# The second products of a feed-forward layer by seven block products in place of eight

## The chip, the cores and the metric

The kernel runs on one core of a Trainium2 chip. TensorE (PE) multiplies, with its weight loads (PEld) beside it; VectorE (DVE), ScalarE (ACT) and GpSimd (POOL) work on SBUF and PSUM; SyncE (SP) issues the DMAs between DRAM and SBUF. Each engine runs its own row of instructions in order, and semaphores tie the rows together. The metric is the device time of one execution of the whole kernel in microseconds, as the median of several runs.

## The reference

One layer of a model, in float32, for 1024 tokens of width 1024: a mixing block, a cross attention, a gated feed-forward and a last norm. Only the feed-forward and the norm bear on this change:

```python
u = rmsnorm(h, norm_ffn_g[l])
h = h + (jax.nn.silu(u @ ffn_w1[l]) * (u @ ffn_w3[l])) @ ffn_w2[l]
...
return rmsnorm(h, norm_final_g)
```

`ffn_w1` and `ffn_w3` are 1024 by 2816, `ffn_w2` is 2816 by 1024. The products `u @ ffn_w1` and `u @ ffn_w3` are called the first products here, the one with `ffn_w2` the second. Silu is x times sigmoid(x).

## The kernel before

All large products are made of pairs: a float32 block is split in a high part (a copy, rounded to the matmul's format, on ScalarE, L281 in `split`) and a low part (the difference, on POOL, L285, or on VectorE), and `mm3` (L298) issues three matmuls for two such pairs: high by high (L299), high by low (L300) and low by high (L301). A matmul of the feed-forward is 128 by 128 by 512 columns.

The hidden width 2816 is 22 blocks of 128 (`FT`), in two halves of 11 (`HF`). Tokens are two halves of 512, columns of the output two halves of 512.

**First products.** They are made by a scheme of seven block products in place of eight (Strassen's idea in Winograd's form): `products(f, A)` for f = 0 to 10 takes weight blocks of the hidden blocks f and f + 11, forms sums of them on VectorE (L1993 to L1997), and computes seven products (P1, P2, P7, P6, P5, P4, P3), each for both weights, 14 products of 12 matmuls in a step f. Results land in PSUM (one pool of eight banks for everything in the feed-forward, `psum`), and VectorE combines them to four blocks (L1989 to L2018). For f = 0 and 1 two of the products are done earlier and kept in SBUF (tag `kept`, eight buffers). `gated` (L1945) takes a sigmoid (ScalarE, L1949), multiplies (VectorE, L1950) and stores the gated hidden block to the DRAM scratch `hid_d` (SP, L1952), four blocks a step. A step also loads 16 weight tiles of 256 KB into a ring of ten (`raw`, tag `wraw`, L1875); their split parts stand in rings of seven (tags `wh` and `wl`). The five sums of the normed tokens which the products use fill both rings `th` and `tl`, of 20 tiles each, and give them back as the last step's products end.

**Second products.** They run plainly: for each token half h, for each column half c, four PSUM accumulators (tile `acc`, one for 128 tokens each) sum over all 22 hidden blocks; that makes 2 x 2 x 22 x 4 x 3 = 1056 matmuls. Hidden blocks are loaded from `hid_d` once for each h (L2045, into `tl` or, for the last eight, `al`), copied for the high part on ScalarE (L2046) and subtracted for the low part on POOL (L2047). Weights come by `raw`, and are split as before. The last three hidden blocks of a pass are done row tile by row tile (`ILAST`), so that the four accumulators end one after the other. After a pass, VectorE adds accumulator and residual (L2087), ScalarE squares with a sum (L2089), POOL multiplies by the gain (L2091), and after the second column half the norm's factor is made (L2095) and applied (`finish`, L2078 to L2082).

**What sets the order.** A scheduler orders each engine's row by the program's order, by priorities and by a clock that it simulates; so code written late can come early in the rows where its inputs are there. All DMAs spoken of here are issued by SP, in one order, and each waits for the one that was issued eight before it.

Of the kernel before, what the change touches and what calls it, by code (L numbers as in the profile page):

```python
# [183 lines left out]
def tile_trunk(ctx, tc, x, mem, norm_mix_g, w_in, rw_mu, rw_w0, rw_w2, rw_a0, rw_a2, rw_g2,  # L184
# [1686 lines left out]
    hd = scratch("hid_d", [FT, NHALF, P, HALF])  # L1871
    def raw(src, k, c, kn, cn):
# [20 lines left out]

    def blocks():

        return [[fp.tile([P, HALF], F32, tag=t, name=f"h{t}", bufs=4 if t == "s" else 2) for t in ts] for ts in (("u2", "u3"), ("c", "s"))
                for _ in range(2)]
# [47 lines left out]
    def gated(n, C, s, f, t):  # L1945

        if n == 0:
            s = fp.tile([P, HALF], F32, tag="s", name="s", bufs=4)
            nc.scalar.activation(s, C, AF.Sigmoid)  # L1949
        nc.vector.tensor_tensor(s, C, s, op=ALU.mult)  # L1950
        if n:
            nc.sync.dma_start(out=hd[f, t], in_=s)  # L1952
        return s

# [74 lines left out]
    next(late)  # L2029
    for f in range(HF):  # L2030
        products(f, weights(f))

    fg = fp.tile([P, D], F32, name="fg", bufs=1)
    nc.sync.dma_start(out=fg, in_=norm_final_g.partition_broadcast(P))
    order = [f + e for f in range(HF) for e in (0, HF)]
    ILAST = 3
    for h in range(NHALF):
        a = act(act1)
        hid = []
        for n, f in enumerate(order):  # L2040
            if n >= FT - KT:
                hh, hl = (t[:, n - FT + KT, :] for t in a)
            else:
                hh, hl = (ring.tile([P, HALF], F32R, tag=t, name=t) for t in ("th", "tl"))
            nc.sync.dma_start(out=hl.bitcast(F32), in_=hd[f, h])  # L2045
            nc.scalar.activation(hh, hl.bitcast(F32), AF.Copy)  # L2046
            nc.gpsimd.tensor_tensor(hl, hl.bitcast(F32), hh.bitcast(F32), op=ALU.subtract)  # L2047
            hid.append((hh, hl))
        hs = blocks()
        for i in range(4):  # L2050
            for c in range(2):
                nc.sync.dma_start(out=hs[i][c], in_=h2d[(4 * h + i) * P:(4 * h + i + 1) * P, c * HALF:(c + 1) * HALF])
        ss = sp.tile([P, 4, 8], F32, tag="ssf", name="ssf")
        for c in range(2):
            cs = slice(c * HALF, (c + 1) * HALF)
            acc = [psum("acc") for _ in range(4)]
            w2 = []
            for n, f in enumerate(order):
# [66 lines left out]
```

## Time and profile before

| what | value |
| --- | --- |
| median of 3 runs | 2398.14 us (2397.16 to 2399.48) |
| the profiled execution | 2398.55 us, its span 2396.8 us |
| granted TensorE clock | 0.993 |
| TensorE busy | 97% of the span |
| second products, first to last matmul | 2139.3 to 2389.9 us of the span |

A page of the profile gives busy time by engine; a window gives the same for a stretch; a row of a timeline gives start and duration of an instruction and, in brackets, how long its engine was idle before it and what released it. Lines such as L2046 are those of the kernel before.

### The profile page before, as it was taken

How to read it: one execution, taken by the hardware profiler on the slowest of the kernel's cores; microseconds unless marked ns; L12 is line 12 of the kernel's file. 1: busy time of each engine (PE TensorE's matmuls, PEld its weight loads, DVE VectorE, ACT ScalarE, POOL GpSimd, SP SyncE). 2: the span in 40 equal slices, each digit the busy share in tenths (PEclk: the TensorE clock that was granted, in tenths of full speed). 3: DMA queues.
4: the chain of work that ended last, by engine and by line, in shares of the span. 5: the costliest groups of instructions: out<-in, count | busy, mean ns of one | idle time of the engine just before them, and what ended most of it. 6: DMA issues, size and time to landing. Idle time of an engine off the chain costs nothing. (4 is left out here: it accounts for less than half of the span.)

```text
span 2396.8 us, 48780 instructions
## 1 busy us (share of the span) xinstructions
PE 2335.8 (97%) x19258; PEld 1934.3 (81%) x19258; DVE 1411.2 (59%) x2288; ACT 1128.3 (47%) x2249; POOL 1228.8 (51%) x1268
## 2 busy tenths in 40 slices
PE   7999999999999999999998999999999999999998
PEld 5777777778887878888887998889778888877887
DVE  5887874667777667767754525444687565640101
ACT  6545454646566656555663415444433333343332
POOL 3554545555466555665664511112565444477673
PEclk9999999999999999999999999999999999999999
DMA  5444445333344343434244823133723223265441
GB/s 168 122 127 121 123 117 161 74 101 85 92 109 110 82 129 105 123 89 126 56 140 152 300 69 117 53 120 132 259 80 101 84 75 93 71 199 172 158 161 57
DMA packets 386001, 288.46 MB, mean 120 GB/s; under 512 B 106171, under 2 KB 329517, under 8 KB 385773
## 3 DMA queue, kind: packets, MB, share of 16 engines
q1 hardware_dynamic: 383341, 279.58, 39.6%
q0 software_dynamic: 1344, 4.72, 0.5%
q8 instruction: 152, 2.49, 0.4%
q10 hardware_dynamic: 1088, 1.05, 0.1%
q14 instruction: 76, 0.62, 0.1%
HBM read 208.73 MB, written 76.02 MB: 119 GB/s over the span
## 5 line engine op out<-in xcount | busy, mean ns | idle before, releaser
L102 PE MATMUL pproj<-uh,whi 128*128 128x512 f32 x768 | 320.0, 417 | 1.1 <-DVE q L102 1.1
L102 PE MATMUL pproj<-uh,wlo 128*128 128x512 f32 x768 | 300.9, 392 | 2.8 <-POOL wlo L102 2.1
L102 PE MATMUL pproj<-ul,whi 128*128 128x512 f32 x768 | 301.2, 392 | 0.0
L285 POOL TENSOR_TENSOR wl<-wraw,wh 128x512 fp32r<-128x512 f32 x154 | 202.1, 1323 | 133.2 <-ACT wh L281 131.6
L285 POOL TENSOR_TENSOR wlo<-wraw,whi 128x512 fp32r<-128x512 f32 (+1 forms) x86 | 117.9, 1374 | 288.6 <-ACT whi L281 280.7
L102 POOL TENSOR_TENSOR wlo<-wraw,whi 128x512 fp32r<-128x512 f32 x96 | 129.0, 1355 | 118.8 <-ACT whi L102 103.8
L281 ACT ACTIVATE whi<-wraw 128x512 fp32r<-128x512 f32 (+1 forms) x166 | 101.0, 617 | 173.1 <-PE pw L301 62.0
L299 PE MATMUL pproj<-uh,whi 128*128 128x512 f32 (+1 forms) x432 | 179.5, 416 | 0.9 <-ACT whi L281 0.6
L281 ACT ACTIVATE wh<-wraw 128x512 fp32r<-128x512 f32 x154 | 94.3, 627 | 182.2 <-PE P L300 74.5
L301 PE MATMUL pproj<-uh,wlo 128*128 128x512 f32 (+1 forms) x432 | 171.4, 397 | 1.5 <-POOL wlo L285 1.5
L102 PEld LDWEIGHTS pproj<-uh,whi 128*128 128x128 f32 x768 | 144.4, 188 | 34.3 <-DVE q L102 2.4
L300 PE MATMUL pproj<-ul,whi 128*128 128x512 f32 (+1 forms) x432 | 170.7, 395 | 0.0
L102 PEld LDWEIGHTS pproj<-ul,whi 128*128 128x128 f32 x768 | 144.3, 188 | 32.0
L102 PEld LDWEIGHTS pproj<-uh,wlo 128*128 128x128 f32 x768 | 144.9, 189 | 28.1 <-POOL wlo L102 2.5
L285 POOL TENSOR_TENSOR wlT<-wraw,whT 128x512 fp32r<-128x512 f32 x70 | 96.6, 1386 | 96.2 <-ACT whT L281 92.5
L299 PE MATMUL pw<-whi,ah 128*128 128x256 f32 x512 | 144.6, 282 | 0.0
L300 PE MATMUL pw<-wlo,ah 128*128 128x256 f32 x512 | 144.6, 282 | 0.0
L301 PE MATMUL pw<-whi,al 128*128 128x256 f32 x512 | 144.3, 282 | 0.0
L2087 DVE TENSOR_TENSOR hu<-acc,hu 128x512 f32<-128x512 f32 x8 | 5.5, 692 | 200.0 <-PE acc L301 200.0
L285 DVE TENSOR_TENSOR wlo<-wraw,whi 128x512 fp32r<-128x512 f32 x80 | 73.7, 922 | 83.4 <-ACT whi L281 83.1
L102 ACT ACT_TABLE_LOAD x90 | 115.5, 1283 | 13.5 <-DVE m L102 6.4
L299 PEld LDWEIGHTS pproj<-uh,whi 128*128 128x128 f32 (+1 forms) x432 | 81.6, 189 | 25.4 <-issue 6.2
(457 smaller groups left out, 6656.2 us busy)
## 6 DMA issues: line engine op xcount, KB each, us to landing
wraw<-in_ffn_w_dram SPq DMA_DIRECT2D x192, 256.0 KB
wraw<-in_w_in_dram SPq DMA_DIRECT2D x148, 256.0 KB
hid_d<-s SPq DMA_DIRECT2D x44, 256.0 KB
tok<-in_x_dram SPq DMA_DIRECT2D x16, 512.0 KB
ar_d<-AR SPq DMA_DIRECT2D x32, 256.0 KB
bk_d<-BK SPq DMA_DIRECT2D x16, 512.0 KB
AR<-ar_d SPq DMA_DIRECT2D x64, 128.0 KB
BK<-bk_d SPq DMA_DIRECT2D x16, 512.0 KB
```

What stands on the lines that cost most here:

```text
L102: r = getattr(self.engine, op)(*a, **kw)
L281: nc.scalar.activation(hi, src, AF.Copy)
L285: e.tensor_tensor(lo, src, hi.bitcast(F32), op=ALU.subtract)
L299: nc.tensor.matmul(ps, ah, bh, start=first, stop=False)
L300: nc.tensor.matmul(ps, ah, bl, start=False, stop=False)
L301: nc.tensor.matmul(ps, al, bh, start=False, stop=last)
L2087: sums.append(nc.vector.tensor_tensor(o, acc[i], o, op=ALU.add).ins.name)
```

## The change

The second products, too, are made by seven block products. Hidden blocks f and f + 11 are the two halves of the inner dimension, so the operands are two by two: tokens by hidden, hidden by columns. Four sums of the gated hidden blocks are made in each step f (`hidden_sums`) and stored to a new DRAM scratch `hsum_d`; four sums of blocks of `ffn_w2` are made for each f (`weight_sums`) and stored to `wsum_d`. Of the four gated blocks of a step only three are stored themselves now. The pool of the `s` tiles has six buffers, where four were.

```diff
     def gated(n, C, s, f, t):
 
         if n == 0:
-            s = fp.tile([P, HALF], F32, tag="s", name="s", bufs=4)
+            s = fp.tile([P, HALF], F32, tag="s", name="s", bufs=6)
...
         if n:
-            nc.sync.dma_start(out=hd[f, t], in_=s)
+            hid[f, t] = s
+            if (f, t) != (f % HF, 1):
+                nc.sync.dma_start(out=hd[f, t], in_=s)
...
+    def hidden_sums(f):
+        x11, x21, x12, x22 = (hid.pop(k) for k in ((f, 0), (f, 1), (f + HF, 0), (f + HF, 1)))
+        s3 = fp.tile([P, HALF], F32, tag="c", name="S3h")
+        nc.gpsimd.tensor_tensor(s3, x11, x21, op=ALU.subtract)
+        tt(x21, x21, x22, op=ALU.add)
+        tt(x11, x21, x11, op=ALU.subtract)
+        nc.gpsimd.tensor_tensor(x12, x12, x11, op=ALU.subtract)
+        for n, t in enumerate((x21, x11, s3, x12)):
+            nc.sync.dma_start(out=hsd[n, f], in_=t)
+
+    def weight_sums(f):
+        y = {}
+        for r in range(2):
+            for c in range(2):
+                y[r, c] = t = fp.tile([P, HALF], F32, tag="kept", name=f"y{r}{c}", bufs=8)
+                nc.sync.dma_start(out=t, in_=ffn_w2[0, (f + r * HF) * P:(f + r * HF + 1) * P, c * HALF:(c + 1) * HALF])
+        t3 = fp.tile([P, HALF], F32, tag="kept", name="T3w", bufs=8)
+        nc.gpsimd.tensor_tensor(t3, y[1, 1], y[0, 1], op=ALU.subtract)
+        nc.gpsimd.tensor_tensor(y[0, 1], y[0, 1], y[0, 0], op=ALU.subtract)
+        tt(y[1, 1], y[1, 1], y[0, 1], op=ALU.subtract)
+        tt(y[1, 0], y[1, 1], y[1, 0], op=ALU.subtract)
+        for n, t in enumerate((y[0, 1], y[1, 1], t3, y[1, 0])):
+            nc.sync.dma_start(out=wsd[n, f], in_=t)
...
+    summed = iter(range(HF))
     for f in range(HF):
         products(f, weights(f))
+        if f >= AHEAD:
+            for _ in range(2 if f < 2 * AHEAD else 1):
+                weight_sums(next(summed))
+        hidden_sums(f)
```

The loops of the second products become seven passes, each over 11 hidden blocks, with four accumulators: 7 x 11 x 4 x 3 = 924 matmuls. A pass has its hidden operand, its weight operand and what is done with its accumulators. The low part of a hidden block is VectorE's now. The residual is loaded in eight DMAs of 512 KB into the tiles that held `ah` and `al`, which the hidden blocks don't use any more.

```diff
+    def p1(i, acc):
+        nc.scalar.activation(U[i], acc, AF.Copy)
+        more(0, i, 0, U[i])
+
+    def p6(i, acc):
+        tt(U[i], acc, U[i], op=ALU.add)
+
+    def p5(i, acc):
+        tt(V[i], acc, U[i], op=ALU.add)
+        more(0, i, 1, V[i])
+        more(1, i, 1, V[i])
+
+    def p7(i, acc):
+        tt(U[i], acc, U[i], op=ALU.add)
+        more(1, i, 0, U[i])
+        add(1, i, 1, acc, ALU.add, True)
...
+    for x, y, then in ((lambda f: hd[f, 0], w2(0, 0), p1),
+                       (lambda f: hd[f + HF, 0], w2(1, 0), lambda i, acc: add(0, i, 0, acc, ALU.add, True)),
+                       (lambda f: hsd[1, f], wsum(1), p6),
+                       (lambda f: hsd[0, f], wsum(0), p5),
+                       (lambda f: hsd[3, f], w2(1, 1), lambda i, acc: add(0, i, 1, acc, ALU.add, False)),
+                       (lambda f: hsd[2, f], wsum(2), p7),
+                       (lambda f: hd[f + HF, 1], wsum(3), lambda i, acc: add(1, i, 0, acc, ALU.subtract, False))):
+        acc = [psum("acc") for _ in range(4)]
+        ops = []
+        for f in range(HF):
+            hh, hl = (ring.tile([P, HALF], F32R, tag=t, name=t) for t in ("th", "tl"))
+            nc.sync.dma_start(out=hl.bitcast(F32), in_=x(f))
+            nc.scalar.activation(hh, hl.bitcast(F32), AF.Copy)
+            tt(hl, hl.bitcast(F32), hh.bitcast(F32), op=ALU.subtract)
+            ops.append((hh, hl, *operand(y(f), "2")))
```

`more` adds a tile to the residual's on POOL, `add` is the old sum, square and gain of an accumulator, and `finish` stands as before but for one product, which VectorE does for the first token half.

The first place where rows move is SP's row in step 2 of the first products, between its weight loads (`wraw`) and its stores of gated blocks (`s`). Before:

```order
L1952 DMA hid_d_20188<-s_21122 128x512
L1875 DMA wraw_21371<-in_ffn_w3_dram 128x4x128
L1952 DMA hid_d_20188<-s_21250 128x512
L1875 DMA wraw_21665<-in_ffn_w1_dram 128x4x128
L1952 DMA hid_d_20188<-s_21293 128x512
L1875 DMA wraw_21667<-in_ffn_w1_dram 128x4x128
L1875 DMA wraw_21669<-in_ffn_w1_dram 128x4x128
L1952 DMA hid_d_20188<-s_21334 128x512
```

And after the change, from behind the last weight load of w3:

```order
L1976 DMA y00_21741<-in_ffn_w2_dram 128x512
L1983 DMA wsum_d_20190<-T3w_21732 128x512
L1983 DMA wsum_d_20190<-y01_21726 128x512
L1976 DMA y01_21743<-in_ffn_w2_dram 128x512
L1983 DMA wsum_d_20190<-y11_21730 128x512
L1976 DMA y10_21745<-in_ffn_w2_dram 128x512
L1976 DMA y11_21747<-in_ffn_w2_dram 128x512
L1983 DMA wsum_d_20190<-y10_21728 128x512
L1976 DMA y00_22074<-in_ffn_w2_dram 128x512
L1983 DMA wsum_d_20190<-T3w_21749 128x512
L1951 DMA hid_d_20188<-s_21267 128x512
L1983 DMA wsum_d_20190<-y01_21743 128x512
```

Four loads of the first group of weight sums stand just ahead of these rows. The loads and stores of the groups alternate, and stand between the weight loads and the gated blocks' stores; in steps 2, 3 and 4 all eleven groups pass.

The second place is POOL's row at the same steps, where `wl` and so on are low parts of weights. Before:

```order
L285 TENSOR_TENSOR wl22_21338<-wraw_21063,wh22_21337 128x512
L285 TENSOR_TENSOR wl11_21374<-wraw_21357,wh11_21373 128x512
L285 TENSOR_TENSOR wl11_21393<-wraw_21365,wh11_21392 128x512
L285 TENSOR_TENSOR wl12_21412<-wraw_21359,wh12_21411 128x512
L285 TENSOR_TENSOR wl12_21434<-wraw_21367,wh12_21433 128x512
L285 TENSOR_TENSOR wlT3_21465<-wraw_21361,whT3_21464 128x512
```

And after:

```order
L285 TENSOR_TENSOR wl22_21355<-wraw_21081,wh22_21354 128x512
L1978 TENSOR_TENSOR T3w_21732<-y11_21730,y01_21726 128x512
L285 TENSOR_TENSOR wl11_21434<-wraw_21417,wh11_21433 128x512
L1979 TENSOR_TENSOR y01_21726<-y01_21726,y00_21724 128x512
L285 TENSOR_TENSOR wl11_21453<-wraw_21425,wh11_21452 128x512
L285 TENSOR_TENSOR wl12_21472<-wraw_21419,wh12_21471 128x512
L1978 TENSOR_TENSOR T3w_21749<-y11_21747,y01_21743 128x512
L1979 TENSOR_TENSOR y01_21743<-y01_21743,y00_21741 128x512
L285 TENSOR_TENSOR wl12_21494<-wraw_21427,wh12_21493 128x512
L285 TENSOR_TENSOR wlT3_21524<-wraw_21421,whT3_21523 128x512
```

Two sums of each of two groups stand among the low parts there; a sum that waits for its load holds the low parts behind it.

The third place is ScalarE's row at the end of the first products, up to the sigmoid of the last step's C22 (`s`); `th` are high parts of hidden blocks, `wh2` those of `ffn_w2`. Before, the end of that stretch, in which sixteen copies of hidden blocks stand ahead of the sigmoid:

```order
L2046 ACTIVATE th_23875<-tl_23876 128x512
L281 ACTIVATE wh22_23801<-wraw_23527 128x512
L2046 ACTIVATE th_23880<-tl_23881 128x512
L281 ACTIVATE wh2_23942<-wraw_23940 128x512
L2046 ACTIVATE th_23885<-tl_23886 128x512
L2046 ACTIVATE th_23890<-tl_23891 128x512
L281 ACTIVATE wh2_23960<-wraw_23958 128x512
L2046 ACTIVATE th_24794<-tl_24795 128x512
L2046 ACTIVATE th_24799<-tl_24800 128x512
L1949 ACTIVATE s_23714<-C22_23712 128x512
```

And after, where ten stand ahead of it:

```order
L2160 ACTIVATE th_24287<-tl_24288 128x512
L2160 ACTIVATE th_24310<-tl_24311 128x512
L2160 ACTIVATE th_24321<-tl_24322 128x512
L281 ACTIVATE wh22_24052<-wraw_23779 128x512
L281 ACTIVATE wh2_24133<-wraw_24131 128x512
L281 ACTIVATE wh2_24156<-wraw_24154 128x512
L1946 ACTIVATE s_23965<-C22_23963 128x512
```

The last copies stand directly ahead of the sigmoid before, and three weight copies behind the last of them after the change.

129 lines of the change are left out of this document (67 added, 62 removed).

## The prediction

> **What bounds the kernel now.** I read the head of the page first, then the stretches of TensorE, then the waits at the place where the first products of the feed-forward end and the second ones begin, and at last the end of the timeline.
>
> ```profile
> span 2396.8 us, 48780 instructions
> PE 2335.8 (97%) x19258; PEld 1934.3 (81%) x19258; DVE 1411.2 (59%) x2288; ACT 1128.3 (47%) x2249; POOL 1228.8 (51%) x1268
> L2087 DVE TENSOR_TENSOR hu<-acc,hu 128x512 f32<-128x512 f32 x8 | 5.5, 692 | 200.0 <-PE acc L301 200.0
> ```
>
> TensorE is busy 97% of the span, and VectorE waits 200 us of the last stage for TensorE's accumulators. The share is an average, so I ask the stage itself. The first window below holds TensorE's instructions in the first products, the other three those of tile acc alone, which is the second products; the columns are window, sum, busy time with instructions, granted clock, DMA share, GB/s.
>
> ```profile
> core 0: us, PE busy (x), PEclk, DMA share, GB/s
> 1906.80:2098.80 192.00, 192.00 (x841) 1.00 0.27 83
> 2139.30:2186.00 46.70, 39.91 (x168) 1.00 0.65 214
> 2186.00:2382.00 196.00, 196.00 (x856) 1.00 0.39 126
> 2382.00:2389.90 7.90, 7.84 (x34) 1.00 0.20 77
> ```
>
> The first window is five steps f of the first products (a step is 14 products of 12 matmuls, and 5 x 168 = 840), so a step takes 38.4 us at full clock and TensorE has no gap in it. The second products begin at 2139.3 and end at 2389.9. Past 2186 they too have no gap: 196.00 / 856 = 0.2290 us a matmul. Only the first 46.7 us do: 168 matmuls at 0.229 are 38.5 us, so **8.2 us** are lost there. The rows of that place:
>
> ```profile
> ACT th L2046 <- DMA tl<-hid_d: 14.2, 2, 12.0
> PE acc L300 <- POOL wl L285: 3.3, 3, 1.9
> PE acc L299 <- DVE C L2010: 3.3, 1, 3.3
> 2135.26 1.32 ACT L2046 ACTIVATE th<-tl 128x512 fp32r<-128x512 f32 x2 [2.79 <-DMA tl<-hid_d]
> 2136.48 0.61 ACT L1949 ACTIVATE s<-C 128x512 f32<-128x512 f32 x1
> 2137.13 6.47 DVE L1950 TENSOR_TENSOR s<-C,s 128x512 f32<-128x512 f32 x1 [10.19 <-ACT s L1949]
> 2143.52 0.68 DVE L2008 TENSOR_TENSOR U<-P,U 128x512 f32<-128x512 f32 x1
> ```
>
> ScalarE stands in hidden copies (th) that wait for loads; behind them in its row stands a sigmoid (s), on it VectorE's product, and only behind that, at 2143.52, the sum that empties a PSUM bank the new accumulators want. Elsewhere a matmul taken out is worth its 0.229 us.
>
> **The change, term by term.** *Removed:* seven passes of 11 blocks by 4 row tiles by 3 matmuls are 924 matmuls where 1056 stood. 132 x 0.229 = **30.2 us**. All matmuls in it have the same shape, so the price is the row's own.
>
> *The end* keeps its form: last matmul, sum, square, rstd, product, store.
>
> ```profile
> 2389.45 0.40 PE L301 MATMUL acc<-wh,al 128*128 128x512 f32 x1
> 2393.61 0.38 SPq L2082 DMA_DIRECT2D out_dram<-hs  x1
> ```
>
> The last store is issued 3.7 us after the last matmul's end at 2389.9 (2389.45 + 0.40), and the span ends 6.9 us after it. I leave it at 6.9. The profiled execution took 2398.55 us, 1.75 more than its span, and lies 0.41 above the median of the three runs (2398.14), so I count against it. With nothing lost: 2139.3 + 924 x 0.229 + 6.9 + 1.75 = **2359.5**.
>
> *The transition.* ScalarE's row, whose end is shown in the part on the change, has ten hidden copies before the sigmoid of step 10 where sixteen stood, and their low parts are VectorE's now and no longer POOL's (whose wait for wl is the 3.3 us above). Fewer loads must land ahead of the sigmoid; but VectorE takes ten more differences just where it is late. Ten at 0.69 are 6.9 us, spread over the last step. The bounds are 0 and the 8.2 us of now; a loss below zero can't be. The wait was for copies six of which are gone, so I take **2**, nearer to none.
>
> *Evictions and sums between passes.* Of the seven passes, each 132 x 0.229 = 30.2 us, every one leaves four banks while the next uses the other four, so an eviction has a whole pass. POOL has 11 splits at 1.30, 14.3 us, and at most 8 sums at 1.30, 10.4 us: 24.7 of 30.2. VectorE has 11 differences: even at the 1.76 us of a paired one (row below), 19.4 us. ScalarE has 22 copies at 0.66 (1.32 / 2), 14.5 us. Each fits, at 0; if POOL's eight sums after one pass all came ahead of the splits, and none were ready, it would be 10.4 us once. I take 0, for the splits run several operands ahead. The loads are 22 blocks of 0.262 MB in 30.2 us, 191 GB/s, below the 327 shown further down; the residual's eight 512 KB loads stand ahead of the eleventh hidden block, 4.2 MB / 327 = 12.8 us and a landing of 5.4 (also below), 18 us, where the block is needed after 8 x 12 x 0.229 = 22 us. That is 0, and 5 if they land late.
>
> *The sums, in the first products.* A step gets one group of hidden sums (two on POOL, two on VectorE, four stores for one store less), and eleven groups of weight sums (four loads, two POOL, two VectorE, four stores each) are put by the order into steps 2, 3 and 4 and the boundary before them: about four in step 2, three in each of the next. The prices are these:
>
> ```profile
> L1993 DVE TENSOR_TENSOR T<-wraw 128x512 f32<-128x512 f32 x12 | 8.3, 692 | 29.5 <-POOL wl L285 29.5
> L285 POOL TENSOR_TENSOR wl<-wraw,wh 128x512 fp32r<-128x512 f32 x36 | 46.7, 1298 | 52.6 <-ACT wh L281 52.6
> 1783.71 6.39 POOL L285 TENSOR_TENSOR wl<-wraw,wh 128x512 fp32r<-128x512 f32 x4 [3.14 <-ACT wh L281]
> 1779.36 1.76 DVE L1993 TENSOR_TENSOR T<-wraw 128x512 f32<-128x512 f32 x1 [2.94 <-POOL wl L285]
> 1783.76 1.80 DVE L1994 TENSOR_TENSOR wraw<-wraw 128x512 f32<-128x512 f32 x1
> 1786.19 1.07 DVE L1950 TENSOR_TENSOR s<-C,s 128x512 f32<-128x512 f32 x1
> 1787.18 3.47 DVE L1995 TENSOR_TENSOR wraw<-T,wraw 128x512 f32<-128x512 f32 x2
> ```
>
> Alone, VectorE's sum of two SBUF tiles takes 0.69 and POOL's 1.30. Beside each other both get longer: four of POOL take 6.39, **1.60 each**, with four of VectorE among them. Now POOL has 14 splits a step; with 2 hidden and 6 weight sums it is 22, by 1.60 each 35.2 us of 38.4. In step 2, with four groups, 24 x 1.60 = 38.4: full to the brim. VectorE has 16 such sums, then 24, and 14 from PSUM: 38 x 0.69 = 26.2 us if alone. So by paired durations the sums just fit, but the splits have no room left, and a late load moves TensorE. If the pairs took turns entirely, a step would need 22 x 1.30 + 24 x 0.69 = 45.2 us, over by 6.8 in two steps and by 10.7 in step 2, **24 us** in all, less what seven split operands ahead cover (38.4 / 14 = 2.74 us each, 19 us if the ring is full).
>
> The Trainium skill's page "SBUF — State Buffer", section "🔬 SBUF: two separate sides", speaks against this change: it says that a VectorE operation with two SBUF inputs and a GpSimd one that reads SBUF exclude each other for the whole instruction. By that rule the four pairs at 1783.71 would have taken 4 x 1.30 + 4 x 0.69 = 8.0 us; the trace shows 6.39, so it agrees on the lengthening and not on its full size. By the rule the time is that of the crowding rival below, by the trace's pairs that of my forecast.
>
> DMA, in the same steps, by the highest stretch that I find and by now:
>
> ```profile
> core 0: us, PE busy (x) PEld busy (x) DVE busy (x) ACT busy (x) POOL busy (x), PEclk, DMA share, GB/s
> 2270.00:2290.00 20.00, 20.00 (x90) 16.57 (x89) 4.15 (x4) 11.08 (x20) 18.76 (x16) 1.00 0.92 327
> hid_d<-s SPq DMA_DIRECT2D x44, 256.0 KB
> 2149.64 5.39 DMA al<-hid_d
> ```
>
> A step moved 20 blocks of 256 KB (16 loads, 4 stores). Steps 2 to 3 in the new order have 44 between the same places: 44 x 0.262 MB / 38.4 us = 300 GB/s, against 83 now and 327 at a share of 0.92. It fits with little left. I take **2.5 us** for ports and queue together, between 0 and 24, because the pairs' row is the nearest and it says "just fits".
>
> The sum: 2359.5 + 2 + 2.5 = **2364**.
>
> **The rivals.** *Crowding:* the sums take port and queue away from the splits and loads, in steps 2 to 4. For it: 38.4 of 38.4 and 300 of 327. Against: seven operands ahead, and no gap of TensorE in the first products now. Price 5 to 24 us: 2359.5 + 2 + 5 to 24 = 2366 to 2386.
>
> *Slower, by one mechanism:* the weight sums become a chain through their eight buffers. Nine groups have to pass in three steps, 115.2 / 9 = 12.8 us each, or the weight loads behind them on SP come late. One group by itself is a load (5.39, by the landing above), four POOL instructions with splits between (5.2), two paired VectorE sums (3.5), and a store (5.39): 19.5 us. If only one went at a time, nine groups would lose 9 x (19.5 - 12.8) = 60 us less 19 of ring, 41 us: 2361.5 + 41 = 2403, slower than before by over 0.2%. So it decides from about 19.5 us a group. The order speaks against it: the load y00_21741 of the second group stands ahead of the first group's stores, so two are under way, 9.8 us a group.
>
> *No change:* losses of 30 to 40 us, half of that chain, 2394 to 2403. *The change doesn't do what it says:* the order has 924 rows of acc where 1056 were, so this falls out.
>
> **How the numbers follow.** My forecast, 2358 to 2372 (with 0 to 5 at the transition and 0 to 7 in the first products), has 0.62; crowding beyond that, to 2386, 0.24; a better time than 2358, 0.03 (TensorE's matmuls would have to get faster, or the end shorter); between 2386 and 2393, 0.01; within 0.2% of now (4.8 us, about what measurements of this kernel can tell from no change), 0.05; slower 0.05. Faster is thus 0.90. The range runs from 2358 to 2386 and leaves out 0.14.
>
> **What would show it.** In the changed profile, 924 matmuls of acc, nearly 0.229 each, TensorE without gaps past the first 50 us of the second products; the transition's loss 0 to 5 where it was 8.2, with no wait on a C sum's bank over 3 us. Steps of the first products at 38.4 us, also steps 2 to 4; if crowding is right, these alone are longer, TensorE waits there for POOL's wl or for a weight load, and POOL's mean goes over 1.60. For the chain, POOL would stand at T3w waiting for the y loads, ahead of splits. I am wrong if passes of the second products have gaps at their starts (POOL's sums ahead of splits, or hidden blocks that land late), or if TensorE waits at the end of step 10 for more than now.

## The result and the profile after

The change made the kernel slower. Its median is 2412.12 us of 4 runs (2410.04 to 2416.77), that of the kernel before 2397.65 of 4 (2393.81 to 2399.48); the ratio is 1.0065, with a 95% interval of 1.0046 to 1.0085. The prediction had 2364, with a range up to 2386.

The profiled execution is the longest of the four, 2416.77 us, so the stages below add up to 18.2 us more than before, where the medians are 14.5 apart. The head of its page, to be held against the same two lines of before:

```profile
span 2415.0 us, 49046 instructions
PE 2324.8 (96%) x19126; PEld 1919.3 (79%) x19126; DVE 1549.7 (64%) x2425; ACT 1135.5 (47%) x2271; POOL 1265.5 (52%) x1273
```

132 matmuls are gone (19258 to 19126), but TensorE's busy time has fallen by 11 us only, where 132 at 0.229 would be 30. So the matmuls that are left got longer on the average. The stages show where:

| stage, us of the span | before | after | difference |
| --- | --- | --- | --- |
| up to the first acc matmul | 2139.3 | 2179.1 | +39.8 |
| from there to the last one's end | 250.6 | 228.7 | -21.9 |
| from there to the span's end | 6.9 | 7.2 | +0.3 |

The second products did shrink, though by 21.9 us and not by 39 (250.6 less 924 x 0.229). The first products, on which no matmul was changed, take 39.8 us longer. Three windows of TensorE after the change; the first is of all its instructions, the other two of tile acc alone (window, sum, busy time with instructions, granted clock, DMA share, GB/s):

```profile
1820.00:1980.00 160.00, 136.37 (x538) 0.93 0.65 217
```

```profile
2179.10:2300.00 120.90, 120.90 (x534) 1.00 0.69 233
2300.00:2407.80 107.80, 95.21 (x392) 0.94 0.37 122
```

The first window is steps 2 to 5 of the first products. 160 us hold 700 matmuls at 0.2286; there were 538, so 37 us are lost in this window, nearly all of the 39.8. 23.6 of them (160 - 136.37) are idle time, and **13.4** (136.37 - 538 x 0.2286) are matmuls that took longer: the clock fell to 0.93. In the second products there is no loss at their start, where the kernel before had its 8.2; past 2300 TensorE is idle for 12.6 us, with a lower clock again.

What TensorE and its suppliers wait for in the window from 1820 to 1980 (engine, line, what released it: total us, times, longest):

```profile
POOL T3w L1978 <- DMA y<-in_ffn_w_dram: 28.5, 8, 6.3
DVE y L1980 <- POOL y L1979: 21.5, 5, 10.8
PE P L299 <- DVE U L2033: 10.3, 2, 7.8
POOL S3h L1964 <- DVE s L1947: 9.3, 3, 3.2
PE P L301 <- POOL wlT L285: 7.5, 6, 2.5
POOL wl L285 <- ACT wh L281: 6.6, 2, 3.6
POOL s L1967 <- DVE s L1966: 5.9, 4, 1.8
PE P L301 <- POOL wl L285: 5.4, 4, 2.0
```

TensorE waits for POOL's low parts and for a PSUM sum of VectorE's. Both stand behind sums: POOL's row holds at T3w until a block of `ffn_w2` lands, VectorE's at y until POOL has made its sum. An engine that runs ahead waits for its supplier instead; for ScalarE's copies POOL waits 9.0 us only here (6.6 in the row above, 2.4 for whT). In POOL's timeline after the change, such a hold (start, duration, and in brackets the idle time before it and its releaser):

```profile
1826.11 2.54 POOL L285 TENSOR_TENSOR wl<-wraw,wh 128x512 fp32r<-128x512 f32 x2
1834.94 1.29 POOL L1978 TENSOR_TENSOR T3w<-y,y 128x512 f32<-128x512 f32 x1 [6.28 <-DMA y<-in_ffn_w_dram]
1836.19 1.27 POOL L285 TENSOR_TENSOR wl<-wraw,wh 128x512 fp32r<-128x512 f32 x1
```

The blocks land late because their loads go out late. SP stands at the stores of T3w until POOL has made it (first row, of the window from 1815 to 1985), and the next group's loads stand between one group's stores (the other rows):

```profile
SPq L1983 <- POOL T3w L1978: 25.8, 7, 5.1
1838.73 0.33 SPq L1983 DMA_DIRECT2D wsum_d<-y  x1
1839.11 0.42 SPq L1976 DMA_DIRECT2D y<-in_ffn_w_dram  x1
1840.98 0.32 SPq L1983 DMA_DIRECT2D wsum_d<-y  x1
1841.35 0.93 SPq L1976 DMA_DIRECT2D y<-in_ffn_w_dram  x2
```

The T3w of the group whose last loads these are starts at 1845.53. From the third group on, the last load of a group is issued 3.5 to 4.8 us before its T3w starts. So the groups hang together in a chain: a group's last loads wait for stores of the group before, and these for its sums.

### The profile page after: what moved, and what is told of

Same layout as the page of the kernel before. It is cut to its first block, busy times and chain, and to the rows that moved or that the text cites. A ratio compares the mean times of both kernels' runs of the same rounds, so it can differ in the third digit from the quotient of the medians.

```text
span 2415.0 us, 49046 instructions
## 1 busy us (share of the span) xinstructions
PE 2324.8 (96%) x19126; PEld 1919.3 (79%) x19126; DVE 1549.7 (64%) x2425; ACT 1135.5 (47%) x2271; POOL 1265.5 (52%) x1273
## 5 line engine op out<-in xcount | busy, mean ns | idle before, releaser
L2161 DVE TENSOR_TENSOR tl<-tl,th 128x512 fp32r<-128x512 f32 x77 | 80.3, 1069 | 100.5 <-ACT th L2160 96.3
L281 ACT ACTIVATE wh<-wraw 128x512 fp32r<-128x512 f32 x143 | 86.5, 623 | 96.1 <-PE P L300 55.9
L300 PE MATMUL acc<-wl,th 128*128 128x512 f32 x308 | 122.3, 397 | 7.3 <-POOL wl L285 7.3
L299 PE MATMUL acc<-wh,th 128*128 128x512 f32 x308 | 122.0, 396 | 5.2 <-ACT wh L281 5.2
L285 POOL TENSOR_TENSOR wlT<-wraw,whT 128x512 fp32r<-128x512 f32 x70 | 105.3, 1515 | 41.4 <-ACT whT L281 31.0
```

Source lines behind the costliest of these rows:

```text
L281: nc.scalar.activation(hi, src, AF.Copy)
L285: e.tensor_tensor(lo, src, hi.bitcast(F32), op=ALU.subtract)
L299: nc.tensor.matmul(ps, ah, bh, start=first, stop=False)
L300: nc.tensor.matmul(ps, ah, bl, start=False, stop=False)
L2161: tt(hl, hl.bitcast(F32), hh.bitcast(F32), op=ALU.subtract)
```

## The experiments

All of them are kernels of 1 core, each with a profile. "First acc" is the start of the first matmul of the second products, and so where the first products end; "acc" goes from there to the start of the last one; the ideal is 924 x 0.229 = 211.6. The kernel before ran beside each group on the same chip (2399.93; 2395.24; 2397.71; 2395.23; 2396.85). Times of e9, e10 and e15 are medians of several runs, the others single ones. First acc repeats within some 3 us: it is 2179.1, 2176.5 and 2177.4 in the three kernels that have the change's own first products. The whole time repeats less well: 13 executions of the kernel before, beside e9, lie between 2390.79 and 2402.30. So the readings below go by the stages.

| run | sums in the first products | time | first acc | acc |
| --- | --- | --- | --- | --- |
| the change | split between engines, crowded | 2412.12 | 2179.1 | 228.3 |
| e1 | no weight sums | 2374.72 | 2138.6 | 226.7 |
| e2 | arithmetic of the weight sums alone | 2400.08 | 2163.9 | 226.6 |
| e3 | DMAs of the weight sums alone | 2377.25 | 2142.0 | 225.8 |
| e4 | split, spread | 2404.93 | 2154.6 | 241.0 |
| e5 | VectorE, crowded | 2392.25 | 2155.9 | 226.9 |
| e6 | VectorE, spread | 2386.90 | 2143.3 | 234.2 |
| e7 | as the change; residual sums on VectorE | 2406.59 | 2176.5 | 220.8 |
| e8 | e6 and e7 together | 2379.34 | 2144.2 | 225.6 |
| e9 | e8, last group earlier, stores later | 2372.64 | 2143.9 | 214.6 |
| e10 | e9 with split sums | 2391.25 | 2158.1 | 219.4 |
| e11 | as the change; stores later | 2409.85 | 2177.4 | 223.1 |
| e13 | the change, hidden sums on VectorE | 2411.32 | 2177.3 | 224.6 |
| e14 | the change, weight sums on VectorE | 2397.47 | 2162.9 | 225.2 |
| e15 | e9 with hidden sums split | 2368.60 | 2145.5 | 215.1 |
| e16 | the change, POOL's half of the weight sums alone | 2409.08 | 2173.5 | 226.2 |
| e17 | the change, VectorE's half of the weight sums alone | 2384.79 | 2149.7 | 225.7 |
| e18 | e1 with 18 more VectorE sums in three steps | 2401.49 | 2165.6 | 226.2 |

### Parts of the weight sums (e1, e2, e3) and another order (e4)

e1 takes the calls of `weight_sums` out:

```diff
-        if f >= AHEAD:
-            for _ in range(2 if f < 2 * AHEAD else 1):
-                weight_sums(next(summed))
...
-            nc.sync.dma_start(out=t[:, 0, :], in_=wsd[n, f])
+            nc.sync.dma_start(out=t[:, 0, :], in_=ffn_w2[0, (f + n // 2 * HF) * P:(f + n // 2 * HF + 1) * P, n % 2 * HALF:(n % 2 + 1) * HALF])
```

> Leaves out the weight sums (loads, arithmetic and stores); the three passes that read them load plain blocks of ffn_w2 of the same size. Theory (weight sums hold POOL's and VectorE's rows while their blocks are on the way): the first products end at 2139 to 2146 us of the span instead of 2179, the time is 2371 to 2380 with the second products' own losses left. Rival (hidden sums, or the whole port load): the end of the first products stays past 2160, the time past 2392.

First acc 2138.6: the whole of the 39.8 us hangs on the weight sums. The hidden sums, with their four stores a step and their split between POOL and VectorE, cost nothing by themselves. The same window as above, of e1, and its POOL waits:

```profile
1820.00:1980.00 160.00, 160.00 (x701) 131.23 (x700) 113.75 (x148) 50.88 (x85) 92.38 (x69) 1.00 0.31 101
```

```profile
POOL wl L285 <- ACT wh L281: 38.3, 21, 5.9
POOL wlT L285 <- ACT whT L281: 16.6, 10, 3.0
```

TensorE (first busy column) has no gap, and POOL (fifth) waits for ScalarE again, as one that runs ahead does.

e2 keeps the arithmetic on blocks that are loaded once, and takes the loads and stores of each group away:

```diff
-                y[r, c] = t = fp.tile([P, HALF], F32, tag="kept", name=f"y{r}{c}", bufs=8)
+                if (r, c) in y:
+                    continue
+                y[r, c] = t = fp.tile([P, HALF], F32, tag="kept", name=f"y{r}{c}", bufs=8)
...
-        for n, t in enumerate((y[0, 1], y[1, 1], t3, y[1, 0])):
-            nc.sync.dma_start(out=wsd[n, f], in_=t)
```

> Keeps the arithmetic of eleven groups of weight sums, three a step in steps 1 to 3 and two in step 4, on tiles that are loaded once; no loads or stores for each group; the passes load plain blocks of ffn_w2. Theory (waits for blocks on the way): the first products end at 2139 to 2148. Rival (POOL and VectorE have no time for the sums, the shared port): TensorE waits in steps 2 to 4 as before, and they end past 2160.

2163.9, the rival's number, though no block was on its way. In this kernel all groups share five tiles, so a group's first sum also waits for VectorE's last of the group before it; these waits are 3.8 us in all from 1750 to 1990, and so don't explain the 25. The groups stand at other places than in the change, though, so e2 says that the sums cost without any load under way, and not what share of the 40 us that is.

e3 keeps the loads and the stores:

```diff
-        nc.gpsimd.tensor_tensor(t3, y[1, 1], y[0, 1], op=ALU.subtract)
-        nc.gpsimd.tensor_tensor(y[0, 1], y[0, 1], y[0, 0], op=ALU.subtract)
-        tt(y[1, 1], y[1, 1], y[0, 1], op=ALU.subtract)
-        tt(y[1, 0], y[1, 1], y[1, 0], op=ALU.subtract)
-        for n, t in enumerate((y[0, 1], y[1, 1], t3, y[1, 0])):
+        for n, t in enumerate((y[0, 1], y[1, 1], y[0, 0], y[1, 0])):
```

> Keeps the loads and the stores of the weight sums, leaves out their arithmetic: the loaded blocks are stored as they are. Theory (an instruction that waits holds its engine's row): no engine but SP waits for these blocks, so the first products end at 2139 to 2150. Rival (the DMA queue is too full, weight loads come late): TensorE waits for wraw loads, and they end past 2160.

2142.0, 3.4 us behind e1, hardly more than the 3 us within which first acc repeats. The scheduler puts the DMAs even closer here, as the window of e3 shows (the last two columns are DMA share and GB/s):

```profile
1820.00:1860.00 40.00, 40.00 (x176) 32.84 (x175) 27.37 (x33) 11.11 (x20) 27.01 (x20) 1.00 0.94 317
```

At 317 GB/s and a share of 0.94 TensorE had no gap. The queue was not the bound.

e4 has all the work, with an order: a group's loads behind the stores of the step before, its sums behind the hidden sum of its step, and the third sum in place, so that a group needs four buffers and not five.

```diff
+                behind(nc.sync.dma_start(out=t, in_=ffn_w2[0, (f + r * HF) * P:(f + r * HF + 1) * P, c * HALF:(c + 1) * HALF]).ins, last)
...
+        behind(nc.gpsimd.tensor_tensor(y[0, 0], y[0, 1], y[0, 0], op=ALU.subtract).ins, anchor)
+        nc.gpsimd.tensor_tensor(y[0, 1], y[1, 1], y[0, 1], op=ALU.subtract)
+        tt(y[1, 1], y[1, 1], y[0, 0], op=ALU.subtract)
+        tt(y[1, 0], y[1, 1], y[1, 0], op=ALU.subtract)
...
+        ready = [weight_loads(next(summed), last) for _ in range(0 if f < AHEAD else 2 if f < 2 * AHEAD else 1)]
         products(f, weights(f))
...
+        anchor, last = hidden_sums(f)
+        for k, y in ready:
+            weight_sums(k, y, anchor)
```

> All the work of the change; order edges put the loads of one group (two in steps 2 and 3) behind the hidden sums' stores of the step before, and its sums behind the hidden sum of its own step, some 30 us after the loads; the third weight sum is made in place. Theory: no sum waits for its blocks, the first products end at 2139 to 2148, the time is 2371 to 2382. Rival (too much work in these engines and queues, wherever it stands): the loss of 40 us is spread but stays, past 2395.

First acc is 2154.6, 24 us better than the change and still 16 behind e1, though no POOL sum waits for a load now. So the theory that the waits for blocks alone make the loss fell: it held for more than half of it. A new loss came at the end: step 10's group, on SP ahead of the eleventh hidden block, made TensorE wait 7.4 us for it, and acc grew to 241.

### Which engine (e5, e6), and the residual sums (e7, e8)

e5 is the change with `tt` (VectorE) for the four `nc.gpsimd.tensor_tensor` in `hidden_sums` and `weight_sums`; e6 is the same edit on e4; e7 is the change with one edit in `more`; e8 is e6 and e7.

```diff
     def more(h, i, c, t):
         o = hs[h][:, 2 * i + c, :]
-        nc.gpsimd.tensor_tensor(o, o, t, op=ALU.add)
+        tt(o, o, t, op=ALU.add)
```

> The change with all eight sums of a group, hidden and weight, on VectorE; loads and stores are where the scheduler puts them. Theory now (POOL's and VectorE's rows wait for each other, in turns, in a group that is split between them, and POOL's low parts stand behind): the first products end at 2139 to 2150, the time is 2374 to 2387. Rival (the pair of engines has no time for the sums, whichever does them: VectorE by its paired 1.76 would need 24 x 1.76 + 14 x 0.69 = 52 us a step): they end past 2165 and VectorE is busy nearly all of steps 2 to 4. Older theory (waits for blocks on the way): VectorE now waits for the y loads, PSUM banks come late, and they end at 2155 to 2180.

> The spread order of e4 with all eight sums on VectorE. Theory now: no turn and no wait is left in the first products, they end at 2139 to 2144, where e4 had 2154.6. Rival (no time for the sums): as in e4 or later, 2154 or more.

e5: 2155.9, outside what the theory gave (to 2150), inside what the older one gave. VectorE held 24.6 us at T3w for its loads, and TensorE 14.0 for PSUM banks. It was busy for 133 of the 160 us of the window, so it was not full. e6: 2143.3, as the theory said. So each of the two edits alone takes some 23 us off, and both together 36.

> The change with its sums into the residual (L2119, eight after the fourth pass and four after the sixth) on VectorE in place of POOL, nothing else. Theory for the second products (these sums stand in POOL's row ahead of the low parts that the next pass needs): the 228 us from the first to the last acc matmul become 212 to 216; the first products end at 2179 as before; time 2398 to 2404. Rival (loads come late at pass starts): 225 or more.

> e6 and e7 together, all of the work of the change. By both theories the parts add up: first products to 2139 to 2144, second products 212 to 216 us, tail 7: span 2358 to 2367, time 2360 to 2369. If the lost time of one only moves to the other, over 2380.

e7: acc 220.8, between the 212 to 216 of the theory and the 225 of the rival. In the change, POOL's row at the start of the fifth pass, and TensorE's gap:

```profile
2304.89 8.84 POOL L2119 TENSOR_TENSOR hres<-hres,Vw 128x512 f32<-128x512 f32 x6
2313.69 3.72 POOL L285 TENSOR_TENSOR wl<-wraw,wh 128x512 fp32r<-128x512 f32 x3
```

```profile
2315.00 0.80 PE L300 MATMUL acc<-wl,th 128*128 128x512 f32 x1 [4.96 <-POOL wl L285]
```

Six sums stand ahead of the three low parts that the pass needs first. With them on VectorE this gap is gone. But the one at the last pass stays (4.24 us in e7), and it has another cause, that SP's row of the change shows: the output stores of the first token half (L2111 and L2115) wait in turns for VectorE's and POOL's last steps, and the hidden loads of the last pass (L2159) stand behind them.

```profile
2356.57 0.33 SPq L2111 DMA_DIRECT2D out_dram<-hres  x1
2358.27 0.33 SPq L2115 DMA_DIRECT2D out_dram<-hres  x1
2358.70 2.38 SPq L2143 DMA_DIRECT2D wraw<-wsum_d  x3
2361.17 0.38 SPq L2159 DMA_DIRECT2D tl<-hid_d  x1
```

```profile
2367.16 0.79 PE L299 MATMUL acc<-wh,th 128*128 128x512 f32 x1 [5.20 <-ACT wh L281]
```

e8 kept e4's late group and these stores, and so missed its 212 to 216 with 225.6.

### The last two waits (e9, e11), and the split again (e10)

```diff
-        ready = [weight_loads(next(summed), last) for _ in range(0 if f < AHEAD else 2 if f < 2 * AHEAD else 1)]
+        ready = [weight_loads(next(summed), last) for _ in range(2 if f in (2, 3) else 1 if 0 < f < HF - 1 else 0)]
...
+    def store(h, dst, src):
+        if h == 0:
+            deferred.append((dst, src))
+        else:
+            nc.sync.dma_start(out=dst, in_=src)
...
+        if len(sums) == 8:
+            for dst, src in deferred:
+                behind(nc.sync.dma_start(out=dst, in_=src).ins, load)
```

e9 is e8 with both edits, e11 the change with the stores' edit alone, e10 is e9 with the eight sums split between the engines as in the change.

> All the work of the change: e8 with the eleven groups of weight sums in steps 1 to 9 (two in steps 2 and 3), so that none is left for step 10, and with the output stores of the first token half issued behind the last pass's hidden loads in place of ahead of them. Theory (the rest of the loss is step 10's group on SP ahead of the eleventh hidden block, and output stores that wait on SP ahead of the last passes' loads): the first products end at 2139 to 2144, the second products take 212 to 217 us, time 2360 to 2367. Rival (these waits only uncover others): 2372 to 2380, as e8.

> The change with nothing but the output stores of the first token half put behind the last pass's loads on SP. Theory: the gap of 5 us at the start of the last pass goes, with the low clock behind it: from the first to the last acc matmul 219 to 223 us where the change had 228; the first products end at 2176 to 2180. Rival (POOL's sums into the residual alone make that gap): 227 or more.

> e9 with the hidden and weight sums split between POOL and VectorE as the change has them. If one engine for all sums matters also once they are spread: the first products end 3 to 12 us later than e9's, with POOL waiting for VectorE's sums. If only the crowding of groups mattered: within 3 us of e9's.

e9 is faster than both kernels: 2372.64 us (2367.88 to 2374.97, 4 runs) against 2397.71 (13 runs), a ratio of 0.99 (0.9882 to 0.9918). Its profiled execution is at 2367.88; the median lies 6 us over what was expected at the upper end, at the lower end of the rival's band (2372 to 2380). By stages the theory holds: first acc 2143.9, acc 214.6; but these are of the profiled execution, which is the fastest of the four. The windows of e9, for steps 2 to 5 and for the second products:

```profile
1820.00:1980.00 160.00, 156.22 (x683) 1.00 0.56 185
2143.90:2358.80 214.90, 211.72 (x925) 1.00 0.60 201
```

e11: acc 223.1, 5.2 less than the change, by the stores alone. e10: first acc 2158.1, 14 us later than e9 and so past what either side expected, with a ratio of 0.9979 (0.997 to 0.9989) to before. So the engine that makes the sums matters also when the groups are spread and no sum waits for a load. POOL in e10, and TensorE behind it:

```profile
1842.16 1.29 POOL L285 TENSOR_TENSOR wlT<-wraw,whT 128x512 fp32r<-128x512 f32 x1 [3.02 <-ACT whT L281]
1844.09 1.30 POOL L1964 TENSOR_TENSOR S3h<-s 128x512 f32<-128x512 f32 x1 [0.63 <-DVE s L1947]
1845.34 2.51 POOL L1981 TENSOR_TENSOR y<-y,y 128x512 f32<-128x512 f32 x2
1847.81 2.48 POOL L1982 TENSOR_TENSOR y<-y,y 128x512 f32<-128x512 f32 x2
1850.25 5.09 POOL L285 TENSOR_TENSOR wlT<-wraw,whT 128x512 fp32r<-128x512 f32 x3
```

```profile
1852.01 0.79 PE L301 MATMUL P<-hS,wlT 128*128 128x512 f32 x1 [5.19 <-POOL wlT L285]
```

Five sums in a row, 6.2 us, stand between two low parts, at a moment when the low parts were hardly ahead of TensorE.

### One of them off POOL (e13, e14), one of them back (e15)

e13 and e14 move only the hidden sums, or only the weight sums, of the change to VectorE (two `nc.gpsimd.tensor_tensor` to `tt` each); e15 is e9 with the two hidden sums of POOL back on it.

> The change with only the hidden sums moved off POOL (all four on VectorE); weight sums as in the change. Theory (POOL's row is full when its waits at the head are counted as well: in the 160 us from 1820 it was busy 107.8 and stood 28.5 for y loads and 15.2 for VectorE's part of the hidden sums): this frees some 25 us of POOL's row, the first products end at 2155 to 2170. Rival (the weight groups, split between the engines, are what costs, wherever the hidden sums are): 2172 or more.

> The change with only the weight sums moved off POOL (all four on VectorE); hidden sums split as in the change. Theory (POOL's row): frees some 53 us of it, POOL has slack again and waits for ScalarE's copies, and what is left is VectorE's own waiting for y loads, as in e5: the first products end at 2150 to 2160. Rival (the split hidden sums cost as much): 2163 or more.

> e9 with the hidden sums split between POOL and VectorE as in the change (e1 had them so without a loss). If POOL's row has room for them, it takes work off VectorE, which is busy 36 of 40 us in e9: the first products end at 2139 to 2144 and the time is that of e9 or up to 3 us less. If the split is what hurts in e10: 2148 or later.

e13: 2177.3, no gain, the rival's number. My count, by which any 25 us taken out of POOL's row would be won, fell: in the window POOL was busy 97.4 us, 10 less than in the change, and waited 31.3 us for ScalarE's copies, 22 more, and yet TensorE stood as long. So a row needn't be full to make TensorE wait. e14: 2162.9, between the two bands and 16 us better than the change. VectorE now stands at the loads in POOL's place:

```profile
DVE T3w L1978 <- DMA y<-in_ffn_w_dram: 33.9, 6, 9.7
```

e15: 2145.5, as e9 within 2 us, with 2368.60 us (2366.32 to 2369.83, 4 runs) and a ratio of 0.9883 (0.9866 to 0.9901) to 2395.23. e9 and e15 can't be told apart by these runs. So the hidden sums may stand on either engine, and e10 against e15 leaves 12.6 us to the two weight sums on POOL.

### Waits at the head of a row, or turns at SBUF (e16, e17, e18)

What the weight sums do there was still open: they hold rows until their blocks land, and each VectorE sum of two SBUF tiles lengthens POOL's operations and is lengthened by them. e16 leaves VectorE's half of a weight group out, e17 POOL's half, each with all loads and stores:

```diff
-        tt(y[1, 1], y[1, 1], y[0, 1], op=ALU.subtract)
-        tt(y[1, 0], y[1, 1], y[1, 0], op=ALU.subtract)
```

```diff
-        t3 = fp.tile([P, HALF], F32, tag="kept", name="T3w", bufs=8)
-        nc.gpsimd.tensor_tensor(t3, y[1, 1], y[0, 1], op=ALU.subtract)
-        nc.gpsimd.tensor_tensor(y[0, 1], y[0, 1], y[0, 0], op=ALU.subtract)
...
-        for n, t in enumerate((y[0, 1], y[1, 1], t3, y[1, 0])):
+        for n, t in enumerate((y[0, 1], y[1, 1], y[0, 0], y[1, 0])):
```

> The change without VectorE's half of the weight sums: POOL's two sums, all loads and all stores stay, so POOL's row and its waits for loads are the change's. Port theory (a POOL operation and a VectorE operation with two SBUF inputs take turns; by alone durations a step with three groups needs 22 x 1.30 + 18 x 0.69 = 41.0 us of 38.4, one with four 43.6, over by 10.4 in three steps, and slow matmuls and DMAs on top): first acc 2152 to 2164. Row theory (POOL's waits at T3w, ahead of low parts, make the loss): 2170 or more.

> The change without POOL's half of the weight sums: VectorE's two sums, all loads and all stores stay. Port theory (16 x 1.30 + 24 x 0.69 = 37.4 us of 38.4): first acc 2139 to 2147. Row theory (VectorE now holds its row at the first sum until the block lands, as it did at T3w in e14 and e5): 2154 to 2165.

e16: 2173.5, as the row theory has it. With half of the arithmetic gone, only 5.6 of the 40 us are won, and POOL stands at T3w for as long as in the change:

```profile
POOL T3w L1978 <- DMA y<-in_ffn_w_dram: 29.4, 5, 7.8
```

e17: 2149.7, between the two. POOL's two sums taken away win 29.4 us; 11 us over e1 are left, 3.4 of them the DMAs', while VectorE stands 18.8 us at its first sum.

e18 is e1 with sums that nothing waits for and that wait for nothing:

```diff
+        if 2 <= f <= 4:
+            for _ in range(6):
+                tt(idle[0], idle[1], idle[2], op=ALU.subtract)
```

> e1, which has no weight sums, with 18 more VectorE sums of two SBUF tiles a step in steps 2 to 4 (six behind P2, P6 and P4 each), on three tiles loaded once: no engine waits for their results, and no DMA is added. Port theory (16 x 1.30 + 36 x 0.69 = 45.6 us of 38.4, over by 7.2 a step, with POOL's low parts late): first acc 2160 to 2180, POOL's mean over 1.7 in these steps. Row theory (VectorE's row needs 36 x 0.69 + 14 x 0.69 = 34.5 us of 38.4, and POOL's is untouched): 2139 to 2147.

2165.6, as the port theory has it, though not quite by its way: from 1790 to 1990 TensorE waits for VectorE's PSUM sums (17.6 us), and less for POOL's low parts (2.5), whose mean stayed below 1.7. The groups of POOL and VectorE in the window from 1820 to 1980:

```profile
L285 POOL TENSOR_TENSOR wlT<-wraw,whT 128x512 fp32r<-128x512 f32 x24 | 36.8, 1546 | 14.7 <-ACT whT L281 13.7 <-DMA hsum_d<-S3h 1.0
```

```profile
L2060 DVE TENSOR_TENSOR idle<-idle 128x512 f32<-128x512 f32 x14 | 17.2, 1226 | 0.2
L2029 DVE TENSOR_TENSOR idle<-idle 128x512 f32<-128x512 f32 x12 | 13.8, 1148 | 0.2
L2046 DVE TENSOR_TENSOR idle<-idle 128x512 f32<-128x512 f32 x12 | 10.8, 904 | 0.2
L2042 DVE TENSOR_TENSOR U<-P,U 128x512 f32<-128x512 f32 x8 | 5.5, 684 | 0.0
```

A sum that takes 0.69 us alone took 0.90 to 1.23 on the average of its place, so VectorE's row overflowed at work that would have fitted. The single rows say what lengthened it: of all 54 added sums, the 23 during which POOL did nothing took 0.67 to 0.70 us each, the 31 beside a POOL operation 1.36 on the average and up to 1.78. The sums with a PSUM input, which TensorE waits for, took 0.68 also beside POOL (last row): they come late, and are not longer. Both causes are real: in the change itself most of the loss hangs on POOL's half with its holds (e16 against e17), and where the sums wait for nothing, the turns alone can cost 27 us (e18). How the 16 us of e4 part between the turns and the place of the sums in POOL's row was not separated.

### The price of a gap (e12)

The kernel before, with POOL kept from its low parts for a while in step 5:

```diff
+        if f == 5:
+            idle = fp.tile([P, HALF], F32, tag="kept", name="idle", bufs=8)
+            nc.gpsimd.tensor_tensor(idle, U2[0], U2[0], op=ALU.subtract)
+            for _ in range(19):
+                nc.gpsimd.tensor_tensor(idle, idle, idle, op=ALU.subtract)
```

> The kernel before, with twenty differences of a tile with itself put into POOL's row in step 5 of the first products, in groups of four or five between low parts; nothing else. It leaves TensorE without low parts for a while. If a gap costs its length only: time over before equals the sum of TensorE's gaps in steps 5 to 7. If the granted clock falls behind a gap: it is more by 1.5 to 2.5 us for each gap of 2 us or longer, and the rows behind such gaps have matmuls at 0.43 us apart.

TensorE had one gap. It ended at a PSUM sum of VectorE's (U) and not at a low part, so it did not come about as meant; its price can be read all the same. The rows behind it are (start, duration):

```profile
1945.21 0.77 PE L299 MATMUL P<-hS,wh 128*128 128x512 f32 x1 [4.75 <-DVE U L2008]
1945.77 0.63 PE L300 MATMUL P<-lS,wh 128*128 128x512 f32 x1
1946.20 0.63 PE L301 MATMUL P<-hS,wl 128*128 128x512 f32 x1
...
1949.61 0.59 PE L300 MATMUL P<-lS,wh 128*128 128x512 f32 x1
1950.04 0.39 PE L301 MATMUL P<-hS,wl 128*128 128x512 f32 x1
1950.27 0.39 PE L299 MATMUL P<-hS,wh 128*128 128x512 f32 x1
```

```profile
1940.00:1980.00 40.00, 35.25 (x145) 0.91 0.26 80
```

Behind the gap matmuls start 0.43 us apart, until 1950.04, and then 0.23 again. The window has 145 of them, which is 33.15 us at 0.2286: of the 6.85 us that are lost, 4.75 are the gap and 2.1 the slow ones. First acc is 5.7 us later than in the kernel before. The time was 5.9 us over (2403.58 against 2397.71), which alone would say little, since executions of the kernel before differ by more. That agrees with the second expectation, for this one gap.

## Why the prediction was wrong

**What held.** The matmuls: 924 of them, at 0.227 to 0.229 where no gap is. The end: 7.2 for 6.9. The transition: I took a loss of 2 and it was none, as the window from 2179.1 to 2300 shows; e1, whose first products end at 2138.6 and so leave no more time for the loads than before, has no gap there either. The DMAs: 300 of 327 GB/s did fit, at 3.4 us in e3.

**The step that failed** is the term of the sums in the first products: "I take 2.5 us for ports and queue together, between 0 and 24, because the pairs' row is the nearest and it says 'just fits'". It was 39.8. I had counted POOL's busy time, 35.2 to 38.4 us of 38.4, and had called that full to the brim, but an engine's row is also taken by each wait at its head: 28.5 us at T3w in four steps, all of it ahead of low parts. The full row alone is not what costs, as e13 shows; the holds cost because low parts that TensorE needs next stand behind them.

I had put these waits into one rival only, with a threshold for a whole group (12.8 us are free, slower than before from 19.5), and had set that rival aside because two groups were under way in the order, 9.8 us a group. Measured, the second to the eleventh T3w start from 1812.88 to 1949.76, nine groups at 15.2 us each: the next group's loads did stand ahead of the last stores in SP's row, but not all of them, and the last one went out only 3.5 to 4.8 us before it was needed. That is 9 x 2.4 = 22 us past what was free, near the 23.6 us of gaps; but sums and low parts share a row, so any slowdown would stretch the groups, and the nearness proves nothing by itself. My threshold was too high for two reasons. I took 19 us off for seven split operands ahead, as if the ring had been full when the crowd came. By the rows, POOL had finished one low part more than TensorE had begun products at 1810 and none more at 1820, where the kernel before had three and five. And a gap of TensorE can cost more than its length: in the window to 1980, 13.4 us of slow matmuls came on top of 23.6 of gaps. Nothing in the sum stood for that, though the kernel before shows it, where its first products start with gaps (busy times of PE, PEld, DVE, ACT and POOL; the clock is third from the right):

```profile
1740.00:1780.00 40.00, 37.01 (x152) 29.56 (x153) 32.53 (x41) 17.89 (x31) 26.53 (x19) 0.96 0.34 103
```

**The rivals.** The crowding rival had the right place, steps 2 to 4, and a price (5 to 24) that was short, since it had neither the holds nor the slow matmuls. The slower rival was right in the sign that it named, POOL at T3w ahead of low parts, and in the outcome; it had 0.05. And e16, with this chain and only half of the arithmetic, has 34.9 of the 40.5 us that the change has over e1. The loss was not the chain of loads alone, though: with the same loads e14, which moves only the weight sums to VectorE, wins 16 us, and e4, where no POOL sum waits for a load, still has 16 over e1.

**The port.** I took 1.60 us for a POOL operation beside VectorE from the four at 1783.71, and held 6.39 us against the 8.0 that the Trainium skill's "SBUF — State Buffer", section "🔬 SBUF: two separate sides", would give them if the two engines exclude each other. That reading stopped too early: the last of the four VectorE sums ran to 1787.18 + 3.47 = 1790.65, so four pairs took 6.94, 1.73 each. By the rule e18's three steps are 21.6 us too long; it was 27.0 us later than e1, with the slow matmuls behind its gaps in that. So it agrees with the rule far better than with a sum that just fits. By the same durations e16 would have needed 10 us more than its steps have, and lost 35: there the rule is not what decides.

**The second products** lost 17 us that I had put at 0. "The splits run several operands ahead" failed at the fifth pass, where six of POOL's eight residual sums came first; I had named 10.4 us for just that and had not taken it. The output stores on SP at the last pass were in none of my terms: I counted the loads' bytes there, and not what else stands in SP's row and waits. e7 and e11 take the one and the other away (7.5 and 5.2 us), e9 both, and 3.0 of the 17 are left.

## What to carry to other kernels

In a row in order, an instruction that waits holds all that stands behind it, and the shares of busy time don't show that. Before work with an operand that is still under way is put into such a row, ask what stands behind it and for how long, ask what its loads themselves wait for in SP's row, and put them a whole step ahead. Where POOL's low parts are hardly ahead of TensorE, give extra sums to VectorE, and spread them, for the two engines slow each other (e18). And price a long gap of TensorE at its length plus the slow matmuls behind it.

## What the runs showed of the hardware

A gap of TensorE can halve its rate for some us afterwards. In the change, gaps of 7.81, 2.50, 2.46, 2.13 and 2.04 us were each followed by matmuls 0.43 us apart, for 3 to 6 us, some at once, some from 1.3 us behind the gap; one of 1.77 us was not. The rows of the shortest one that was:

```profile
1953.96 0.79 PE L301 MATMUL P<-hB,wl 128*128 128x512 f32 x1 [2.04 <-POOL wl L285]
1954.55 0.63 PE L299 MATMUL P<-hB,wh 128*128 128x512 f32 x1
1954.98 0.63 PE L300 MATMUL P<-lB,wh 128*128 128x512 f32 x1
```

The Trainium skill's page "TensorE: Matmul & The Clock Gate", section "🔬 Part 1: The HAM clock gate (the "warmup" mystery)", has the halved rate, and puts it behind an idle window of about 3.4 us. The rows agree on the halved rate (0.43 for 0.23 us); in them 2.04 us were enough, where the last gap before had ended 16 us earlier. But the length of a gap alone doesn't decide it: the kernel before has a gap of 3.35 us ahead of the matmul at 2144.85, and the matmuls behind it are 0.23 us apart. Counted from 1790 us on in all twenty kernels, each of the 35 gaps above 3.5 us had slow matmuls within 5 us behind it, and about 30 of the 43 gaps from 2 to 3.4 us had them. What decides for the others is open.
